# A two-layer trunk with mixture-of-experts: the dispatch steps around an expert's transposes, a later branch, a shorter rejoin of x1 and full-width norms

## The chip, the cores and the metric

The kernel runs on one core of a Trainium2 chip. The metric is the device time of one execution in microseconds (us), as a median over runs; lower is better.

## The reference

Two layers; each is a token mixer (layer 0: forgetting attention beside an S5 scan, layer 1: mLSTM) and a hierarchical mixture of experts, each followed by a layer norm of `ALPHA * h + branch`. There are 512 tokens of width 1024, 16 experts with a hidden width of 256, and two experts per token. The change touches the mixture and the norm behind it, and by shared helpers every norm:

```
for layer in range(DEPTH):
    h = layer_norm(DN_ALPHA * h + mix, ln_g[layer, 0], ln_b[layer, 0])
    ffn = hier_moe(h, ...)                       # two of 16 experts for each token
    h = layer_norm(DN_ALPHA * h + ffn, ln_g[layer, 1], ln_b[layer, 1])
...
hid = silu(t @ w_gate[e]) * (t @ w_up[e])        # 1024 -> 256, for each expert e
out = sum over e of combine[t, e] * (hid @ w_down[e])   # 256 -> 1024
layer_norm: (x - mean) * rsqrt(var + 1e-5) * g + b
```

## The kernel before

Numbers are kept as two parts. Every fp32 operand is split into a high part (a cast on ACT) and a low part (source minus high part, on DVE or POOL), and each product is three matmuls, high·high, high·low and low·high (`mm3`, L266 to L268). An expert's weights are three pieces of 1 MB, [128, 2048] fp32: two for gate and up (`gu(e)`, pieces 3e and 3e+1) and one for the down product (piece 3e+2). SP loads a piece (L247) into `raw` or one of two `ca` buffers, ACT casts the high part (L213), and the low part is subtracted at L214. Of 48 pieces of a layer POOL subtracts the down pieces of experts 1 to 13 and the pieces 42 and 45 (the first gate/up pieces of experts 14 and 15); DVE does the others.

The experts are worked on two by two. A pair (2m, 2m+1) needs the tokens of both gathered as columns: `dispatch` makes one-hot matrices on DVE (L1054, eight [128, 128] comparisons for a pair, in the pool `t`) and multiplies tokens by them on PE (L1073, 64 matmuls for a pair in four steps of 16, into `tp`), and each step's result is split (ACT and DVE, into `s` or `xr`). While a pair is computed, the next pair's dispatch runs as a generator, `prep`: four steps, two in each of the pair's experts.

For an expert e the loop of `experts` runs `gate_up(e)` (24 matmuls of 512 columns into `pj`), two steps of `prep`, then `hidden`: tanh on ACT (L1028), two elementwise steps on DVE (L1029, L1030) into `th`, and two transposes on PE (L1033, tile `sm`). The transposes are split into `pt`, and the down product follows (12 matmuls into `mm`), ACT evacuates it (L1180) into `a` and stores it to `yd` in memory (L1184).

The program is written in this order, and a scheduler decides from it, from priorities and from free buffers the order of instructions on each engine. Each engine then runs its own list in order.

At the start of `experts` stands `overflow`: each engine loads the largest count of tokens of an expert and jumps over a block that is needed only above 128 (L1210, L1211). With the last pair behind it, `gather` rebuilds `ALPHA * x1` from its two parts (`xs`, L1196 on ACT and L1197 on DVE) into `xr` and adds the stored rows of `yd` to it with eight indirect transfers of POOL (L1201). Experts 14 and 15 are not stored: their products are added from PE (L1282, L1284). `ln_sums` then does the norm of each block of 128 tokens in two halves of 512 columns: sums, Square on ACT (L314), small steps (L316, L317, L319), Identity on ACT (L323) and two steps by halves on DVE (L324, L325) of which a few go to POOL by `LN_POOL`.

Of the kernel before, what the change touches and what calls it, by code (L numbers as in the profile page):

```python
# [23 lines left out]
TWO_PI = 6.283185307179586  # L24
S5_AT = 1, 1, 2
QK_AT = 1, 3
LN_POOL = (), (0,), (0,), ()
NLAST = 2


# [21 lines left out]
class Trunk:  # L52
# [242 lines left out]
    def ln_apply(self, y, gb, mu, rs):  # L295
        V = self.nc.vector
        g, b = gb
        for i in range(2):
            h = np.s_[:, i * 512:(i + 1) * 512]
            V.scalar_tensor_tensor(y[h], y[h], mu, g[h], op0=ALU.subtract, op1=ALU.mult)  # L300
            V.scalar_tensor_tensor(y[h], y[h], rs, b[h], op0=ALU.mult, op1=ALU.add)

    def ln_sums(self, y, s, gb, pool):

        nc = self.nc
        V = nc.vector
        g, b = gb
        mu = self.sm("lnmu", [128, 1], bufs=4)
        V.tensor_scalar(mu, s[:, 0:1], s[:, 1:2], -1.0 / 1024, op0=ALU.add, op1=ALU.mult)
        yield  # L310
        q = self.sm("lns", [128, 2], bufs=4)
        for i in range(2):
            junk = self.t("t", [128, 512])
            nc.scalar.activation(junk, y[:, i * 512:(i + 1) * 512], AF.Square, bias=mu, accum_out=q[:, i:i + 1])  # L314
        ve = self.sm("lnve", [128, 1])
        V.tensor_scalar(ve, q[:, 0:1], q[:, 1:2], 1.0 / 1024, op0=ALU.add, op1=ALU.mult)  # L316
        V.tensor_scalar(ve, ve, EPS, None, op0=ALU.add)  # L317
        rs = self.rstd(ve)
        V.tensor_tensor(mu, mu, rs, op=ALU.mult)  # L319
        yield  # L320
        for i in range(2):
            h = np.s_[:, i * 512:(i + 1) * 512]
            self.last_act = nc.scalar.activation(y[h], y[h], AF.Identity, scale=rs, bias=mu)  # L323
            self.last_ln = V.tensor_tensor(y[h], y[h], g[h], op=ALU.mult)  # L324
            (nc.gpsimd if i in pool else V).tensor_tensor(y[h], y[h], b[h], op=ALU.add)  # L325
        yield


# [556 lines left out]
    def route(self, tb, layer, gb, lT, mu, rs, first):  # L885
# [77 lines left out]
                               op0=ALU.mult, op1=ALU.mult, accum_out=es)  # L963
        V.tensor_tensor(es, es, gs, op=ALU.mult)
        V.reciprocal(es, es)
        V.tensor_scalar(se, se, es, None, op0=ALU.mult)
        def scatter(r, deps=False):
            ins = nc.gpsimd.indirect_dma_start(
                out=self.cd[:, :], out_offset=bass.IndirectOffsetOnAxis(ap=pos[:, r:r + 1], axis=0),
# [47 lines left out]
    def moe_piece(self, base, i, j):  # L1017

        return self.load_piece([128, 2, 1024] if i % 3 == 2 else [128, 4, 512], *self.MOE_TAGS[j % 2],
                               "raw2" if j == 3 else self.MOE_RAW[(j - (j > 3)) % 3], at=base + i,  # L1020
                               eng=self.nc.gpsimd if i % 3 == 2 and 2 < i < 42 or i in (42, 45) else None,
                               deps=self.routed if j == 3 else (None, self.routed[1]) if j in (1, 2) else None)

    def hidden(self, gu):

        nc = self.nc
        th = self.t("t", [128, 256])
        nc.scalar.activation(th, gu[:, 0:256], AF.Tanh, scale=0.5)  # L1028
        nc.vector.scalar_tensor_tensor(th, th, 1.0, gu[:, 0:256], op0=ALU.add, op1=ALU.mult)  # L1029
        nc.vector.scalar_tensor_tensor(th, th, 0.5, gu[:, 256:512], op0=ALU.mult, op1=ALU.mult)  # L1030
        tp = self.p("sm", [128, 2, 128])
        for k in range(2):
            nc.tensor.transpose(tp[:, k, :], th[:, k * 128:(k + 1) * 128], self.ident)  # L1033
        return tp

    def tok_T(self, x):
# [91 lines left out]
    def experts(self, layer):  # L1128
        nc = self.nc
        yd = self.yd[0:2048, :].rearrange("(p e) d -> e p d", e=16)  # L1130
        base = self.piece_i
        x = []
        self.banked = []
        self.onehots(self.oh3, 3)
        self.overflow(layer, base)
        for _ in self.pair_parts(0, x):
            pass
        self.flush()
        self.sources()
        cb = self.sm("s5bc", [128, 256], bufs=1)  # L1140
        nc.sync.dma_start(cb, self.cd[0:2048, :].rearrange("(p e) c -> p (e c)", e=16))
        back, last, gus, xs, used = [], [], {}, {0: x}, iter(range(48))
        prep = None

        def gate_up(e):
            es = slice((e % 2) * 128, (e % 2 + 1) * 128)
            gus[e] = gu = self.p("pj", [128, 512])
            for q in range(2):
                w = self.moe_piece(base, 3 * e + q, next(used))
                for k in range(4):  # L1150
                    xk = xs[e // 2][q * 4 + k]
                    self.mm3(gu, xk, w, q == 0 and k == 0, q == 1 and k == 3, np.s_[:, es], np.s_[:, k, :])

        for e in range(16):
            if e % 2 == 0 and e < 14:
                xs[e // 2 + 1] = []
                prep = self.pair_parts(e // 2 + 1, xs[e // 2 + 1], back if e == 12 else None)
            if e < 15:
                gate_up(e)
            if e == 14:  # L1160
                gate_up(15)
            for _ in range(2):
                next(prep, None)
            tp = self.hidden(gus.pop(e))
            hT = (self.t("pt", [128, 2, 128], F32R), self.t("pt", [128, 2, 128], F32R))
            self.split(hT[0], hT[1], tp)
            w = self.moe_piece(base, 3 * e + 2, next(used))
            c = cb[:, 17 * e:17 * e + 1]
            if e < 16 - NLAST:
                yo = self.t("a", [128, 1024])  # L1170
            else:
                yo = (self.t("a", [128, 1024], F32R), self.t("a", [128, 1024], F32R))
                last.append(yo)
            for n in range(2):
                ns = np.s_[n * 512:(n + 1) * 512]
                ps = self.p("mm", [128, 512])
                for k in range(2):
                    self.mm3(ps, hT, w, k == 0, k == 1, np.s_[:, k, :], np.s_[:, k, ns])
                if e < 16 - NLAST:
                    nc.scalar.activation(yo[:, ns], ps, AF.Copy, scale=c)  # L1180
                else:
                    self.split(yo[0][:, ns], yo[1][:, ns], ps, scale=c)
            if e < 16 - NLAST:
                nc.scalar.dma_start(yd[e], yo)  # L1184
            if e == 15 - NLAST:
                self.gather()
                gb = self.load_ln(2 * layer + 1)
        self.piece_i += 48
        return back, last, gb

    def gather(self):

        nc = self.nc
        for tb in range(4):
            self.xr[tb] = self.t("xr", [128, 1024])
            nc.scalar.activation(self.xr[tb], self.xs[tb][0].bitcast(F32), AF.Copy, scale=ALPHA)  # L1196
            nc.vector.scalar_tensor_tensor(self.xr[tb], self.xs[tb][1].bitcast(F32), ALPHA, self.xr[tb],  # L1197
                                           op0=ALU.mult, op1=ALU.add)
        for r in range(2):
            for tb in range(4):  # L1200
                nc.gpsimd.indirect_dma_start(  # L1201
                    out=self.xr[tb], out_offset=None, in_=self.yd[:, :],
                    in_offset=bass.IndirectOffsetOnAxis(ap=self.src[:, tb, r:r + 1], axis=0),
                    compute_op=ALU.add)
# [64 lines left out]
    def moe(self, layer, done):  # L1269
# [3 lines left out]
        for tb in range(6):  # L1273
            if tb < 4:
                x = self.xr[tb]
                s = self.sm("lnsm", [128, 2], bufs=4)
                for n in range(2):
                    ns = np.s_[n * 512:(n + 1) * 512]
                    ps = self.p("pj" if n == 0 else "mm", [128, 512])
                    for i in range(NLAST):  # L1280
                        for j in range(2):
                            nc.tensor.matmul(ps, lhsT=back[i][:, tb * 128:(tb + 1) * 128], rhs=last[i][j][:, ns],  # L1282
                                             start=i + j == 0, stop=i == NLAST - 1 and j == 1)
                    nc.vector.scalar_tensor_tensor(x[:, ns], ps, 1.0, x[:, ns], op0=ALU.mult, op1=ALU.add,  # L1284
                                                   accum_out=s[:, n:n + 1])
                ln.append(self.ln_sums(x, s, gb, LN_POOL[tb]))
                next(ln[tb])
            if 0 < tb < 5:
                next(ln[tb - 1])
            if tb > 1:  # L1290
                next(ln[tb - 2])
                if tb == 2 and layer == 0:
                    self.prefetch([128, 8, 256], deps=(self.last_act, self.last_ln))
                done(tb - 2, self.xr[tb - 2])
# [304 lines left out]
```

## Time and profile before

| | |
|---|---|
| time, three runs | 1133.0, 1134.22, 1135.67 us; median 1134.22 us |
| the profiled execution | 1129.98 us, span 1127.9 us |
| mean granted clock of TensorE | 0.966 of full speed |
| busy share of the span | PE 91%, DVE 72%, ACT 50%, POOL 34% |
| experts of layer 0 | about 319 to 541 us of the span |
| experts of layer 1 | about 875 to 1102 us, then the last norm until the end |

PE is TensorE, DVE VectorE, ACT ScalarE, POOL GpSimd, and SP the queue that issues the weight loads. A row of a timeline gives the start in us from the span's start, the duration, engine, line, operation, output<-inputs and shapes; what stands in brackets at its end is the idle time of the engine just before it, and what ended it. The granted clock is the share of full speed that the chip allowed TensorE: matmuls of 512 columns then start 0.23 us apart, at half speed 0.43 us.

### The profile page before, as it was taken

Reading aid. Unit: us, or ns where it says so; the run is one execution under the profiler, and the core shown is the slowest. Engines: PE = TensorE matmul, PEld = TensorE weight load, DVE = VectorE, ACT = ScalarE, POOL = GpSimd, SP = SyncE. Lnnn points to the kernel's source line nnn. Section 1 sums busy time; section 2 is a strip of 40 time slices with the busy share of each in tenths; the row PEclk is TensorE's granted clock in tenths of the full one; section 3 lists DMA queues with packets and bytes.
Section 4 is the critical chain, followed back from the end, with each engine's and each line's share of the span. In section 5 each row is a group of like instructions: output and inputs, shape, how many; then the busy total and the mean of one; then the engine's idle time right before and its main releaser. Section 6 shows DMA issues by size and latency. Waiting matters only on the chain. (4 is left out here: it accounts for less than half of the span.)

```text
span 1127.9 us, 14810 instructions
## 1 busy us (share of the span) xinstructions
PE 1022.9 (91%) x5522; PEld 826.9 (73%) x5522; DVE 815.3 (72%) x1485; ACT 559.5 (50%) x778; POOL 379.6 (34%) x226
## 2 busy tenths in 40 slices
PE   7879999999989999997699999999999899999872
PEld 5566767767768787875577989898777787877761
DVE  7886899778776776767665766667988767767666
ACT  5123554461445665664544444444424556666744
POOL 3077546001223333345243333331012233424352
PEclk9899999999989999999799999999999899999986
DMA  6313321541257786768622222221402577868684
GB/s 227 104 58 109 127 66 46 170 170 37 114 211 249 274 291 233 287 240 248 144 75 75 76 75 75 75 76 38 150 38 114 178 267 274 313 226 297 226 218 134
DMA packets 48347, 180.62 MB, mean 160 GB/s; under 512 B 17588, under 2 KB 18516, under 8 KB 32264
## 3 DMA queue, kind: packets, MB, share of 16 engines
q1 hardware_dynamic: 41240, 156.11, 39.4%
q0 software_dynamic: 2992, 8.77, 4.0%
q10 hardware_dynamic: 4032, 14.68, 3.2%
q8 instruction: 46, 0.75, 0.3%
q14 instruction: 37, 0.30, 0.1%
HBM read 155.94 MB, written 22.42 MB: 158 GB/s over the span
## 5 line engine op out<-in xcount | busy, mean ns | idle before, releaser
L266 PE MATMUL pj<-x,wh 128*128 128x512 f32 x288 | 116.6, 406 | 7.4 <-ACT x L213 5.7
L214 POOL TENSOR_TENSOR wl<-raw,wh 128x2048 fp32r<-128x2048 f32 x15 | 69.9, 4663 | 137.2 <-ACT wh L213 137.2
L267 PE MATMUL pj<-x,wh 128*128 128x512 f32 x288 | 115.5, 401 | 0.0
L214 POOL TENSOR_TENSOR wl<-ca,wh 128x2048 fp32r<-128x2048 f32 x16 | 75.1, 4692 | 119.9 <-ACT wh L213 97.5
L213 ACT CAST wh<-raw 128x2048 fp32r<-128x2048 f32 (+1 forms) x49 | 88.2, 1801 | 53.4 <-DMA raw<-in_w 40.0
L268 PE MATMUL pj<-x,wl 128*128 128x512 f32 x288 | 114.7, 398 | 0.0
L1073 PEld LDWEIGHTS tp<-t,a 128*128 128x128 f32 x896 | 110.8, 191 | 3.0 <-ACT pt L1065 0.6
L1073 PE MATMUL tp<-t,a 128*128 128x256 f32 x896 | 111.8, 283 | 0.0
L214 POOL TENSOR_TENSOR x<-ca,x 128x2048 fp32r<-128x2048 f32 x14 | 64.6, 4618 | 135.7 <-ACT x L213 106.2
L214 DVE TENSOR_TENSOR wl<-raw,wh 128x2048 fp32r<-128x2048 f32 (+1 forms) x34 | 72.8, 2140 | 39.6 <-ACT wh L213 39.3
L214 DVE TENSOR_TENSOR wl<-ca,wh 128x2048 fp32r<-128x2048 f32 x14 | 32.1, 2292 | 60.7 <-ACT wh L213 60.7
L1180 ACT ACTIVATE a<-mm,s5bc 128x512 f32<-128x512 f32 x56 | 38.5, 687 | 73.4 <-PE mm L268 73.4
L213 ACT CAST x<-ca 128x2048 fp32r<-128x2048 f32 (+1 forms) x40 | 66.1, 1651 | 12.3 <-DMA ca<-in_w 8.4
L266 PEld LDWEIGHTS pj<-x,wh 128*128 128x128 f32 x288 | 55.4, 192 | 19.7 <-ACT x L213 6.8
L267 PEld LDWEIGHTS pj<-x,wh 128*128 128x128 f32 x288 | 54.8, 190 | 12.0 <-DVE x L214 1.8
L213 ACT CAST wh<-ca 128x2048 fp32r<-128x2048 f32 x30 | 57.1, 1904 | 13.0 <-DMA ca<-in_w 12.9
L268 PEld LDWEIGHTS pj<-x,wl 128*128 128x128 f32 x288 | 55.1, 191 | 10.7
L1054 DVE TENSOR_SCALAR t<-iota,rcm 128x128 fp32r<-128x128 f32 x112 | 58.5, 565 | 0.4
L267 PE MATMUL pj<-wl,x 128*128 128x256 f32 x192 | 56.4, 294 | 0.9 <-DVE wl L214 0.9
L268 PE MATMUL pj<-wh,x 128*128 128x256 f32 x192 | 56.2, 293 | 0.1
L266 PE MATMUL pj<-wh,x 128*128 128x256 f32 x192 | 56.2, 293 | 0.0
L281 POOL TENSOR_TENSOR lnrs<-lnve,nhalf 128x1 f32<-128x1 f32 x16 | 13.1, 818 | 126.3 <-DVE lnve L292 99.7
(488 smaller groups left out, 2869.1 us busy)
## 6 DMA issues: line engine op xcount, KB each, us to landing
raw<-in_w SPq DMA_DIRECT2D x63, 1024.0 KB, 5.2
ca<-in_w SPq DMA_DIRECT2D x62, 1024.0 KB, 5.8
yd<-a ACTq DMA_DIRECT2D x28, 512.0 KB
a<-in_ln SPq DMA_DIRECT2D x8, 512.0 KB, 6.5
a<-in_w SPq DMA_DIRECT2D x6, 512.0 KB, 6.8
yd<-t SPq DMA_DIRECT2D x6, 512.0 KB, 3.1
ca<-in_xT SPq DMA_DIRECT2D x8, 256.0 KB, 5.7
xr<-in_x SPq DMA_DIRECT2D x4, 512.0 KB, 6.3
```

What stands on the lines that cost most here:

```text
L213: a = nc.scalar.copy(h, src)
L214: b = (eng or nc.vector).tensor_sub(l, src, h.bitcast(F32))
L266: nc.tensor.matmul(ps, lhsT=aH[ai], rhs=bH[bi], start=first, stop=False)
L267: nc.tensor.matmul(ps, lhsT=aH[ai], rhs=bL[bi], start=False, stop=False)
L268: nc.tensor.matmul(ps, lhsT=aL[ai], rhs=bH[bi], start=False, stop=last)
L281: self.last_pow = self.nc.gpsimd.tensor_tensor(rs, ve, self.nhalf, op=ALU.pow)
L1054: ins = nc.vector.tensor_scalar(oh[:, j, m * 128:(m + 1) * 128], self.iota1, c[2 * i + j], None, op0=ALU.is_equal)
L1073: nc.tensor.matmul(tp[:, k, :], lhsT=self.xs[tb][i][:, cs], rhs=ohs[tb], start=tb + i == 0, stop=tb + i == 4)
L1180: nc.scalar.activation(yo[:, ns], ps, AF.Copy, scale=c)
```

## The change

It has five parts. `hidden` is cut in two, with one step of `prep` between the DVE steps and the transposes, and the other between the split of the transposes and the down product; before, both steps stood ahead of it. The branch of `overflow` is called behind expert 1. `gather` rejoins x1 in one addition on DVE, with ALPHA taken into the stored rows' scale and the norm's epsilon. The norms work on the full width: one Square on ACT, two combined steps on DVE, no Identity on ACT and nothing on POOL. Pieces 42 and 45 go from POOL to DVE.

```
     def ln_apply(self, y, gb, mu, rs):
...
+        V.scalar_tensor_tensor(y, y, mu, g, op0=ALU.subtract, op1=ALU.mult)
+        V.scalar_tensor_tensor(y, y, rs, b, op0=ALU.mult, op1=ALU.add)
...
     def ln_sums(self, y, s, gb):
...
+        junk = self.t("t", [128, 1024], BF16)
+        self.last_act = nc.scalar.activation(junk, y, AF.Square, bias=mu, accum_out=q)
+        V.scalar_tensor_tensor(y, y, mu, g, op0=ALU.add, op1=ALU.mult)
...
+        V.tensor_scalar(ve, q, 1.0 / 1024, EPS / ALPHA ** 2, op0=ALU.mult, op1=ALU.add)
         rs = self.rstd(ve)
-        V.tensor_tensor(mu, mu, rs, op=ALU.mult)
         yield
-            self.last_act = nc.scalar.activation(y[h], y[h], AF.Identity, scale=rs, bias=mu)
-            self.last_ln = V.tensor_tensor(y[h], y[h], g[h], op=ALU.mult)
-            (nc.gpsimd if i in pool else V).tensor_tensor(y[h], y[h], b[h], op=ALU.add)
+        self.last_ln = V.scalar_tensor_tensor(y, y, rs, b, op0=ALU.mult, op1=ALU.add)
...
-                               eng=self.nc.gpsimd if i % 3 == 2 and 2 < i < 42 or i in (42, 45) else None,
+                               eng=self.nc.gpsimd if i % 3 == 2 and 2 < i < 42 else None,
...
-        self.overflow(layer, base)                       # experts, ahead of the first pair
...
-            for _ in range(2):
-                next(prep, None)
-            tp = self.hidden(gus.pop(e))
+            th = self.hidden_act(gus.pop(e))
+            next(prep, None)
+            tp = self.hidden_T(th)
             hT = (self.t("pt", [128, 2, 128], F32R), self.t("pt", [128, 2, 128], F32R))
             self.split(hT[0], hT[1], tp)
+            next(prep, None)
             w = self.moe_piece(base, 3 * e + 2, next(used))
...
+            if e == 1:
+                self.overflow(layer, base)
...
-            nc.scalar.activation(self.xr[tb], self.xs[tb][0].bitcast(F32), AF.Copy, scale=ALPHA)
-            nc.vector.scalar_tensor_tensor(self.xr[tb], self.xs[tb][1].bitcast(F32), ALPHA, self.xr[tb],
-                                           op0=ALU.mult, op1=ALU.add)
+            nc.vector.tensor_tensor(self.xr[tb], self.xs[tb][0].bitcast(F32), self.xs[tb][1].bitcast(F32), op=ALU.add)
```

Below stands what this does to the lists of DVE and PE in the pair (4, 5) of layer 0. On DVE before, from expert 4's steps (`t_4430`) to the one-hots of the next dispatch (`t_4616`), which come behind expert 5's first step:

```order
L214 TENSOR_TENSOR x_934_4468<-ca_4466,x_933_4467 128x2048
L214 TENSOR_TENSOR wl_4486<-raw_4484,wh_4485 128x2048
L214 TENSOR_TENSOR s_917_4406<-tp_4388,s_916_4405 128x512
L1029 SCALAR_TENSOR_TENSOR t_4430<-t_4430,pj_4341 128x256
L1030 SCALAR_TENSOR_TENSOR t_4430<-t_4430,pj_4341 128x256
L214 TENSOR_TENSOR s_920_4427<-tp_4409,s_919_4426 128x512
L214 TENSOR_TENSOR pt_4438<-sm_4434,pt_4437 128x256
L214 TENSOR_TENSOR wl_4582<-ca_4580,wh_4581 128x2048
L1029 SCALAR_TENSOR_TENSOR t_4544<-t_4544,pj_4465 128x256
L1054 TENSOR_SCALAR t_4616<-iota_130,rcm_2778 128x128
L1030 SCALAR_TENSOR_TENSOR t_4544<-t_4544,pj_4465 128x256
L1054 TENSOR_SCALAR t_4616<-iota_130,rcm_2778 128x128
```

On DVE in the changed kernel, at the same two weight pieces and expert 4's steps (now `t_4370`, L1024 and L1025; the one-hots are `t_4374` and `t_4379`, L1052):

```order
L213 TENSOR_TENSOR x_934_4460<-ca_4458,x_933_4459 128x2048
L213 TENSOR_TENSOR wl_4478<-raw_4476,wh_4477 128x2048
L1024 SCALAR_TENSOR_TENSOR t_4370<-t_4370,pj_4333 128x256
L1052 TENSOR_SCALAR t_4374<-iota_130,rcm_2776 128x128
L1025 SCALAR_TENSOR_TENSOR t_4370<-t_4370,pj_4333 128x256
L1052 TENSOR_SCALAR t_4374<-iota_130,rcm_2776 128x128
L1052 TENSOR_SCALAR t_4374<-iota_130,rcm_2917 128x128 x2
L1052 TENSOR_SCALAR t_4379<-iota_130,rcm_3059 128x128 x2
L1052 TENSOR_SCALAR t_4379<-iota_130,rcm_3262 128x128 x2
L213 TENSOR_TENSOR pt_4409<-sm_4405,pt_4408 128x256
```

The run of eight one-hots has moved from the odd expert to the even one, to just behind (and around) the steps whose result PE transposes. On PE before, at expert 4's transposes (`sm_4434`; the dispatch ahead of them ends with `tp_4409`, and its one-hots `t_4378` and `t_4383` were made in the pair before):

```order
L1073 MATMUL tp_4409<-t_4383,a_3235 128x256
L1073 MATMUL tp_4409<-t_4383,a_3236 128x256
L266 MATMUL pj_4465<-x_933_4467,xr_4171 128x512
L267 MATMUL pj_4465<-x_934_4468,xr_4171 128x512
L268 MATMUL pj_4465<-x_933_4467,xr_4172 128x512
L266 MATMUL pj_4465<-x_933_4467,xr_4171 128x512
L1033 MATMUL sm_4434<-ident,t_4430 128x128 x2
L267 MATMUL pj_4465<-x_934_4468,xr_4171 128x512
L268 MATMUL pj_4465<-x_933_4467,xr_4172 128x512
L266 MATMUL pj_4465<-x_933_4467,xr_4171 128x512
L267 MATMUL pj_4465<-x_934_4468,xr_4171 128x512
L266 MATMUL mm_4448<-wh_4442,pt_4437 128x512
```

On PE in the changed kernel, at the same transposes (`sm_4405`), with the last matmuls of gu(5) (`pj_4457`) that are put ahead of them:

```order
L265 MATMUL pj_4457<-wh_4477,xr_4279 128x512
L266 MATMUL pj_4457<-wl_4478,xr_4279 128x512
L267 MATMUL pj_4457<-wh_4477,xr_4280 128x512
L265 MATMUL pj_4457<-wh_4477,xr_4279 128x512
L1031 MATMUL sm_4405<-ident,t_4370 128x128 x2
L1071 MATMUL tp_4384<-t_4374,a_2744 128x256
L1071 MATMUL tp_4384<-t_4374,a_2745 128x256
L1071 MATMUL tp_4412<-t_4374,a_2744 128x256
L1071 MATMUL tp_4384<-t_4374,a_2886 128x256
L1071 MATMUL tp_4384<-t_4374,a_2887 128x256
L1071 MATMUL tp_4412<-t_4374,a_2745 128x256
L1071 MATMUL tp_4384<-t_4379,a_3027 128x256
```

The 32 matmuls of the dispatch now stand between the transposes and the down product (which follows the 32nd of them), and they read the one-hots `t_4374` and `t_4379` that DVE makes in the rows above. Sixteen matmuls of gu(5) stand ahead of the transposes, where there were four. In the odd expert the other two steps (32 matmuls) stand behind the even expert's down product and eight matmuls of gu(5), with four matmuls of gu(6) between them and the transposes. On PE in the changed kernel the branch (L1208, L1209) stands inside the down product of expert 1 (`mm_3559`, `mm_3567`):

```order
L267 MATMUL pj_4099<-wh_4101,s_724_3407 128x512
L265 MATMUL mm_3559<-x_755_3553,pt_3527 128x512
L266 MATMUL mm_3559<-x_756_3554,pt_3527 128x512
L265 MATMUL mm_3567<-x_755_3553,pt_3527 128x512
L1208 TENSOR_LOAD rmc_3285
L1209 COMPARE_AND_BRANCH
```

Before, it stood ahead of the last L1109 matmuls in front of gu(0).

## Rows read from the trace of the kernel before

**Rows 1.** Windows: busy time of each engine in the experts of layer 0.

```profile
320.00:541.00 221.00, 203.06 (x1078) 168.95 (x1077) 147.25 (x183) 131.92 (x142) 84.62 (x24) 0.98 0.75 260
```

**Rows 2.** PE's waits, 312 to 530 us: total, times, longest.

```profile
PE mm L268 <- DVE pt L214: 6.1, 4, 2.1
```

**Rows 3.** Timeline of PE: transposes of experts 2, 4, 6 and 12; one expert's dispatch matmuls.

```profile
357.48 0.38 PE L1033 MATMUL sm<-ident,t 128*128 128x128 f32 x2
...
364.68 3.98 PE L1073 MATMUL tp<-t,a 128*128 128x256 f32 x32
...
382.80 0.38 PE L1033 MATMUL sm<-ident,t 128*128 128x128 f32 x2
...
409.28 0.44 PE L1033 MATMUL sm<-ident,t 128*128 128x128 f32 x2
...
494.24 0.38 PE L1033 MATMUL sm<-ident,t 128*128 128x128 f32 x2
```

**Rows 4.** Timeline of PE at the branch and the start of gu(0), layer 0.

```profile
316.45 0.98 PE L1109 MATMUL mm<-pt,a 128*128 128x256 f32 x3 [3.62 <-PEq L1211]
...
318.94 0.63 PE L266 MATMUL pj<-wh,xr 128*128 128x512 f32 x1
...
321.29 0.40 PE L266 MATMUL pj<-wh,xr 128*128 128x512 f32 x1
...
325.02 0.40 PE L267 MATMUL pj<-x,xr 128*128 128x512 f32 x1
```

**Rows 5.** Lines of DVE, 351 to 489 us (experts 2 to 11).

```profile
L1054 DVE TENSOR_SCALAR t<-iota,rcm 128x128 fp32r<-128x128 f32 x40 | 23.2, 631 | 0.0
```

**Rows 6.** DVE, layer 0: the tile `t` by lines, 300 to 560 us.

```profile
L1054 DVE TENSOR_SCALAR t<-iota,rcm x56: 270/278/3446, 320.9 to 483.7; 128x128 fp32r<-128x128 f32 x56
```

**Rows 7.** Timeline of POOL: subtractions of the down pieces.

```profile
357.11 4.61 POOL L214 TENSOR_TENSOR x<-ca,x 128x2048 fp32r<-128x2048 f32 x1 [11.07 <-DVE t L1030]
369.72 5.75 POOL L214 TENSOR_TENSOR wl<-ca,wh 128x2048 fp32r<-128x2048 f32 x1 [8.00 <-ACT wh L213]
384.87 4.59 POOL L214 TENSOR_TENSOR x<-ca,x 128x2048 fp32r<-128x2048 f32 x1 [9.39 <-ACT x L213]
...
410.21 4.61 POOL L214 TENSOR_TENSOR x<-ca,x 128x2048 fp32r<-128x2048 f32 x1 [7.81 <-ACT x L213]
```

**Rows 8.** Timeline of DVE around one collision with a POOL subtraction.

```profile
368.73 2.29 DVE L214 TENSOR_TENSOR x<-raw,x 128x2048 fp32r<-128x2048 f32 x1
...
372.46 3.10 DVE L1054 TENSOR_SCALAR t<-iota,rcm 128x128 fp32r<-128x128 f32 x1
```

**Rows 9.** Timeline of DVE: the first step of expert 2.

```profile
356.23 0.41 DVE L1029 SCALAR_TENSOR_TENSOR t<-t,pj 128x256 f32<-128x256 f32 x1
```

**Rows 10.** Timeline of PE after a wait of 4 us.

```profile
518.68 0.54 PE L267 MATMUL pj<-x,s 128*128 128x512 f32 x1 [4.00 <-DVE x L214]
...
522.43 0.39 PE L267 MATMUL pj<-x,s 128*128 128x512 f32 x1
```

**Rows 11.** Timeline of DVE in the tail of layer 1.

```profile
1068.39 1.21 DVE L1197 SCALAR_TENSOR_TENSOR xr<-a,xr 128x1024 f32<-128x1024 f32 x1
...
1073.66 6.40 DVE L214 TENSOR_TENSOR x<-raw,x 128x2048 fp32r<-128x2048 f32 x1
...
1109.38 0.69 DVE L1284 SCALAR_TENSOR_TENSOR xr<-pj,xr 128x512 f32<-128x512 f32 x1 [0.73 <-DMA xr<-yd,rsrc]
```

**Rows 12.** Timeline of POOL: the gathers of layer 1.

```profile
1081.79 1.94 POOL L1201 DMA_INDIRECT xr<-yd,rsrc  x1 [3.89 <-DMA yd<-a]
...
1092.67 1.54 POOL L1201 DMA_INDIRECT xr<-yd,rsrc  x1 [3.34 <-DMA xr<-yd,rsrc]
```

**Rows 13.** Lines of DVE, 1109 to 1128 us.

```profile
L324 DVE TENSOR_TENSOR xr<-xr,a 128x512 f32<-128x512 f32 x8 | 5.4, 682 | 0.0
L325 DVE TENSOR_TENSOR xr<-xr,a 128x512 f32<-128x512 f32 x6 | 4.0, 688 | 0.1
L319 DVE TENSOR_TENSOR lnmu<-lnmu,lnrs 128x1 f32<-128x1 f32 x4 | 2.7, 683 | 1.4 <-POOL lnrs L281 1.4
```

More of the change, by code (lines that the diff above doesn't have):

```diff
@@ L26 @@
 QK_AT = 1, 3
-LN_POOL = (), (0,), (0,), ()
 NLAST = 2
@@ L297, in ln_apply, with ln_sums @@
         g, b = gb
[L298 to L303, printed above, removed]
+        V.scalar_tensor_tensor(y, y, mu, g, op0=ALU.subtract, op1=ALU.mult)
+        V.scalar_tensor_tensor(y, y, rs, b, op0=ALU.mult, op1=ALU.add)
+    def ln_sums(self, y, s, gb):
         nc = self.nc
@@ L310, in ln_sums @@
         yield
[L311 to L314, printed above, removed]
+        q = self.sm("lns", [128, 1], bufs=4)
+        junk = self.t("t", [128, 1024], BF16)
+        self.last_act = nc.scalar.activation(junk, y, AF.Square, bias=mu, accum_out=q)
+        V.scalar_tensor_tensor(y, y, mu, g, op0=ALU.add, op1=ALU.mult)
         ve = self.sm("lnve", [128, 1])
-        V.tensor_scalar(ve, q[:, 0:1], q[:, 1:2], 1.0 / 1024, op0=ALU.add, op1=ALU.mult)
-        V.tensor_scalar(ve, ve, EPS, None, op0=ALU.add)
+        V.tensor_scalar(ve, q, 1.0 / 1024, EPS / ALPHA ** 2, op0=ALU.mult, op1=ALU.add)
         rs = self.rstd(ve)
-        V.tensor_tensor(mu, mu, rs, op=ALU.mult)
         yield
-        for i in range(2):
-            h = np.s_[:, i * 512:(i + 1) * 512]
-            self.last_act = nc.scalar.activation(y[h], y[h], AF.Identity, scale=rs, bias=mu)
-            self.last_ln = V.tensor_tensor(y[h], y[h], g[h], op=ALU.mult)
-            (nc.gpsimd if i in pool else V).tensor_tensor(y[h], y[h], b[h], op=ALU.add)
+        self.last_ln = V.scalar_tensor_tensor(y, y, rs, b, op0=ALU.mult, op1=ALU.add)
         yield
@@ L965, in route @@
         V.reciprocal(es, es)
-        V.tensor_scalar(se, se, es, None, op0=ALU.mult)
+        V.tensor_scalar(se, se, es, 1.0 / ALPHA, op0=ALU.mult, op1=ALU.mult)
         def scatter(r, deps=False):
@@ L1020, in moe_piece, with hidden_act @@
                                "raw2" if j == 3 else self.MOE_RAW[(j - (j > 3)) % 3], at=base + i,
-                               eng=self.nc.gpsimd if i % 3 == 2 and 2 < i < 42 or i in (42, 45) else None,
+                               eng=self.nc.gpsimd if i % 3 == 2 and 2 < i < 42 else None,
                                deps=self.routed if j == 3 else (None, self.routed[1]) if j in (1, 2) else None)
     def hidden(self, gu):
+        return self.hidden_T(self.hidden_act(gu))
+    def hidden_act(self, gu):
         nc = self.nc
@@ L1030, in hidden, with hidden_T @@
         nc.vector.scalar_tensor_tensor(th, th, 0.5, gu[:, 256:512], op0=ALU.mult, op1=ALU.mult)
+        return th
+    def hidden_T(self, th):
         tp = self.p("sm", [128, 2, 128])
         for k in range(2):
-            nc.tensor.transpose(tp[:, k, :], th[:, k * 128:(k + 1) * 128], self.ident)
+            self.nc.tensor.transpose(tp[:, k, :], th[:, k * 128:(k + 1) * 128], self.ident)
         return tp
@@ L1285, in moe @@
                                                    accum_out=s[:, n:n + 1])
-                ln.append(self.ln_sums(x, s, gb, LN_POOL[tb]))
+                ln.append(self.ln_sums(x, s, gb))
                 next(ln[tb])
```

## The prediction

> **What bounds the kernel now.** I read the windows first: in the 221 us of layer 0's experts PE is busy for 203 us, at a granted clock of 0.98, and no other engine for more than 147 us [rows 1]. So PE's own list sets the pace, and I read its timeline next. The transposes of expert 2 start at 357.48 and those of expert 12 at 494.24: five pairs in 136.8 us, 27.4 us each [rows 3]. What must PE do in a pair? 72 matmuls of 512 columns (48 for gate and up, 24 for the two down products), which start 0.233 us apart (321.29 to 325.02, 16 steps [rows 4]), 16.8 us; and two groups of 32 dispatch matmuls of 3.98 us [rows 3], 8.0 us. With the transposes about 25 us. So a pair has 2.4 us to lose or win at most, 12 us for a layer's five full pairs. PE's largest wait, 6.1 us in four, is at the third matmul of a down product, for the low part of the transposed hidden values, `pt` [rows 2]. The reader should look at why that part is late.
>
> DVE's lines tell it: 40 one-hot comparisons took 0.631 us on average [rows 5], but the median of the same line is 0.278 us and the longest 3.446 us [rows 6]. So each of the five runs of eight held one blocked comparison: 40 times (0.631 - 0.278) is 14.1 us, 2.8 us for each run. The timeline names the partner. POOL began a subtraction at 369.72 and ended it at 375.47; the comparison that DVE began at 372.46 ended at 375.56 [rows 7, 8]. POOL's own operation took 5.75 us instead of 4.61, because DVE was in a subtraction until 371.02 when it began [rows 7, 8]. Whichever of the two is under way, the other waits for its end.
>
> A page of the Trainium skill, "SBUF — State Buffer", section "Who interferes with whom", says that DVE and GpSimd share one port pair, that a DVE instruction of the tensor_scalar kind or with two SBUF inputs contends for it, and that whoever issues first has it for the whole instruction. By that rule the same run would cost nothing if it were issued first, and POOL would wait instead; the trace shows both orders (3.10 us on DVE, 1.1 us on POOL [rows 7, 8]).
>
> In before this collision is cheap, since the run's one-hots are for the next pair's dispatch; only `pt` queued behind the run is late, in odd experts.
>
> **The dispatch step.** The gain it can have: 32 dispatch matmuls lie between the transposes and the down product, so that `pt` has 4 us to be split and PE's waits of rows 2 go. If nothing else waited, a pair would lie between 25 us (all waits gone) and 27.4 (none); I take 26.0, since only the `pt` waits are addressed: -1.4 us.
>
> But the orders show a new dependence. Those 32 matmuls read one-hots that DVE makes around L1024 and L1025 of the same expert, just ahead of use, where before they had been made in the pair before. So a blocked comparison now stops PE with nothing left to run: the transposes, the dispatch and the down product stand behind it in order. Does POOL's subtraction fall there? In both kernels it waits for ACT's cast of the odd expert's down piece, which ACT runs behind the even expert's tanh. In before's expert 2, DVE's first step starts at 356.23 and POOL at 357.11, 0.9 us later [rows 7, 9]. Placed in the new order from that first step, the run of eight lasts at most to +3.0 us (two steps of 0.41 and eight comparisons of 0.278 [rows 6, 9]); as such operations overlap by some hundredths each, I take +2.3. So POOL begins within the run. Measured from the transposes of the even expert, POOL starts at -0.37 in expert 2, +2.07 in expert 4, and +0.93 in expert 6 [rows 3, 7]; experts 8 and 10 lie between 2 and 6. The transposes come about 1.1 us behind the first step, so that the run would end at about +1.2 from them. Four of five start inside it; expert 4 escapes, because its piece landed late.
>
> Price of one collision: POOL's 4.61 us from a start that lies 0 to 2.3 us into the run, so the run ends 2.3 to 4.6 us late, and I take 3.6 (a start about 1.3 us into it, between the 0.9 of expert 2 and the 2 of expert 6). PE then waits about that long, and it comes back slow: behind the wait of 4.00 us at 518.68 nine matmuls took 3.75 us instead of 2.10 [rows 10], behind that of 3.62 us at the branch the first 2.35 us of gu(0) held 6 matmuls worth 1.40, with the L1109 ahead slower still [rows 4]. So +1.65 to 2.1; I take 1.9. A collision costs 5.5 us (bounds 2.3, where the wait is too short to slow the clock, and 6.7).
>
> Pairs: five per layer from expert 1's down product on, with nothing colliding 5 × -1.4 = -7.0; the sixth run, for the last pair, stands in a stretch where order and tail shift against each other, and I put it at +0.4 without a collision. With 12 possible collisions in the kernel (six a layer), each adds 5.5.
>
> **The branch.** PE's idle time at L1109 is 3.62 us and it runs slow behind it [rows 4]. That stays; it moves. At the start the gain is small, about 2 us, as gu(0) waits for its piece's high and low parts anyway. In expert 1's down product nothing covers it: 3.6 + 1.9 = 5.5 us. Queued behind it are ACT's evacuation, and SP's loads behind its own jump. Net +3.5 us a layer (bounds +1.5, if the piece is not what gu(0) waits for, and +5.5).
>
> **The tail.** The first gather is issued at 1081.79, and the fifth one (1092.67) waited for the first to land [rows 12]; two weight loads, freed late because DVE's subtraction took 6.40 us against POOL's of piece 45, share the memory with it [rows 11]. With piece 45 on DVE and L1196 gone, the subtraction takes 2.3 and the loads precede the gathers. I put the first landing at 5 us behind its issue instead of 10: -4.9 (bounds 0 and -7). The last gather's data is used at 1109.38 [rows 11]; from there DVE works through eight L324, six L325 and four L319, 12.1 us [rows 13]. In their place stand at most seven full-width steps of 1.21 us (the price of L1197, a two-input step of that width [rows 11]), 8.5 us: -3.3 (bounds -2 and -5). The narrow norm ahead of the experts gains 0.7. The rest of gather's ACT work is off the path. Together -8.9 a layer.
>
> **Sum.** Without collisions, a layer: -7.0 + 0.4 + 3.5 - 8.9 = -12.0, the kernel -24. With c collisions: -24 + 5.5c. It breaks even between 4 and 5 of 12. Four of five in the rows above would be 9 or 10; I take 9, since POOL could be held off by a DVE subtraction or a late landing: -24 + 49.5 = +25.5 us. Against the profiled 1129.98 that is 1155.5; this execution lies 4.2 us under the median of the runs, so 1160 for the median.
>
> **Rivals.** *The run goes first (faster).* If the down piece lands late, as in expert 4, or if DVE's back-to-back operations keep POOL out, the one-hots are made before the subtraction and nobody on PE waits: 0 to 2 collisions, -24 to -13, 1110 to 1121. It decides at about 2.3 us from the first step: a POOL start behind that costs nothing. For it speaks expert 4 [rows 3, 7]; against it that the longer pairs of a colliding order give the pieces more time to land. By the page's rule above this is the case of DVE issued first. *The pace is not PE's (faster).* POOL takes a down piece in every 13.3 us on average (357.11 to 410.21, four steps [rows 7]) through one buffer, so load, cast and subtraction could hold a pair at 27.4 whatever PE's order is; then the pairs give 0 in place of -7.0 and nothing collides at cost: -5.0 a layer, 1124. *Half and half.* 4 to 6 collisions: -2 to +9, 1132 to 1143. *All 12 collide at the full 6.7:* -24 + 80 = +56, 1190; at 5.5 it is +42, 1176.
>
> **How the numbers follow.** Most runs collide (7 to 12): 0.57, from 1149 to 1176, likeliest 1160. None or few: 0.22. Pace held elsewhere: 0.11. Half and half: 0.10. About 0.2% (2.3 us) is what a measurement of this kernel can tell from no change; of half and half 0.05 falls inside it, 0.01 below and 0.04 above. So faster 0.34, same 0.05, slower 0.61. The range takes in both signs: 1112 to 1180; for the likeliest case alone 1146 to 1178.
>
> **What would show it.** Right: comparisons at L1052 with a longest of 3 to 4.6 us in the even experts, PE idle 2 to 4 us at the first L1071 matmuls or the L1031 transposes, released by DVE, with a granted clock below 1 behind it, and transposes of even experts about 31 us apart where they collide, 26 where not. PE idle some 3.6 us in expert 1's down product. First gather landing about 5 us after its issue. Wrong: POOL's L213 beginning behind the run, or PE's waits at L1071 under 1 us; then the time ends near 1115. The tail could be mis-sized by 2 to 4 us a layer without touching the sign.

## The result, and the profile after

The changed kernel takes 1195.24 us (median of 4 runs, 1192.04 to 1198.86), the kernel before 1134.95: a ratio of 1.0538, interval 1.0497 to 1.0579. It is slower, as forecast, but by 60 us in place of 25, and outside the range. Ratios and intervals, here and below, are of executions in the usual, faster state; the medians beside them are of all. The profiled execution (span 1197.1 us) holds some 7 us that are not the change's: at 150 to 202 us, in layer 0's mixer, its granted clock was 0.84 where before had 1.00, and work that took before 45 us there took 52. So I read stages, not the span.

The same window as in [rows 1], with the experts some 7 us further on, shows PE busy for 190.64 us in place of 203.06, at a granted clock of 0.90 in place of 0.98:

```profile
320.00:541.00 221.00, 190.64 (x958) 162.30 (x957) 138.01 (x171) 114.40 (x124) 63.69 (x16) 0.90 0.63 225
```

PE's waits in layer 1's experts (900 to 1150 us; total, times, longest). The wait for `pt` of [rows 2] is gone; five waits for one-hots, one for the elementwise steps, one at the transposes of the last pair's one-hots (L1060) and the branch (L1209) stand in its place:

```profile
PE tp L1071 <- DVE t L1052: 18.5, 5, 3.9
PE mm L267 <- PEq L1209: 4.5, 1, 4.5
PE sm L1031 <- DVE t L1025: 3.9, 1, 3.9
PE tp L1060 <- DVE t L1052: 3.6, 1, 3.6
```

One pair, layer 1, expert 6. PE's timeline first, then DVE's and POOL's. POOL (4.56 us) begins half a microsecond after DVE has begun the run of seven comparisons; the run, 1.46 us where nothing holds it, takes 5.72. PE does six dispatch matmuls, stands for 3.78 us, and the other 26 take 4.90 us, where [rows 3] has 3.98 for all 32:

```profile
1027.78 0.38 PE L1031 MATMUL sm<-ident,t 128*128 128x128 f32 x2
1027.92 0.95 PE L1071 MATMUL tp<-t,a 128*128 128x256 f32 x6
1032.65 4.90 PE L1071 MATMUL tp<-t,a 128*128 128x256 f32 x26 [3.78 <-DVE t L1052]
```

```profile
1026.42 0.41 DVE L1024 SCALAR_TENSOR_TENSOR t<-t,pj 128x256 f32<-128x256 f32 x1
1026.75 0.28 DVE L1052 TENSOR_SCALAR t<-iota,rcm 128x128 fp32r<-128x128 f32 x1
1026.94 0.42 DVE L1025 SCALAR_TENSOR_TENSOR t<-t,pj 128x256 f32<-128x256 f32 x1
1027.28 5.72 DVE L1052 TENSOR_SCALAR t<-iota,rcm 128x128 fp32r<-128x128 f32 x7
1032.91 0.41 DVE L213 TENSOR_TENSOR pt<-sm,pt 128x256 fp32r<-128x256 f32 x1
```

```profile
1027.76 4.56 POOL L213 TENSOR_TENSOR x<-ca,x 128x2048 fp32r<-128x2048 f32 x1 [7.29 <-ACT x L212]
```

The transposes of experts 2 and 12 of layer 0 (PE's timeline, as in [rows 3]) are now (524.04 - 371.61) / 5 = 30.5 us apart per pair, in place of 27.4. One run of layer 0 escaped: in expert 4 (403.06) the subtraction began at 403.93, and the comparisons had taken 1.46 us:

```profile
371.61 0.38 PE L1031 MATMUL sm<-ident,t 128*128 128x128 f32 x2
...
403.06 0.38 PE L1031 MATMUL sm<-ident,t 128*128 128x128 f32 x2
...
524.04 0.27 PE L1031 MATMUL sm<-ident,t 128*128 128x128 f32 x1
```

Counted over both layers, 13 of 14 runs (seven a layer, the first pair's included; there it is a small step between the comparisons that is held) were held by a subtraction of POOL.

### The profile page after: what moved, and what is told of

It reads as the page before. It is cut to its first block, busy times and chain, and to the rows that moved or that the text cites. A ratio compares the mean times of both kernels' runs of the same rounds, so it can differ in the third digit from the quotient of the medians.

```text
span 1197.1 us, 14715 instructions
## 1 busy us (share of the span) xinstructions
PE 1055.1 (88%) x5522; PEld 859.4 (72%) x5522; DVE 825.1 (69%) x1445; ACT 538.3 (45%) x738; POOL 355.9 (30%) x218
## 5 line engine op out<-in xcount | busy, mean ns | idle before, releaser
L1071 PE MATMUL tp<-t,a 128*128 128x256 f32 x896 | 137.3, 320 | 25.6 <-DVE t L1052 25.6
L1071 PEld LDWEIGHTS tp<-t,a 128*128 128x128 f32 x896 | 134.0, 228 | 29.1 <-DVE t L1052 27.1
L213 POOL TENSOR_TENSOR wl<-ca,wh 128x2048 fp32r<-128x2048 f32 x12 | 55.2, 4599 | 176.4 <-DVE t L1025 103.2
L213 DVE TENSOR_TENSOR x<-ca,x 128x2048 fp32r<-128x2048 f32 (+1 forms) x26 | 46.6, 1797 | 69.2 <-ACT x L212 69.2
L1052 DVE TENSOR_SCALAR t<-iota,rcm 128x128 fp32r<-128x128 f32 x112 | 71.6, 700 | 0.0
L280 POOL TENSOR_TENSOR lnrs<-lnve,nhalf 128x1 f32<-128x1 f32 x16 | 18.9, 1182 | 134.8 <-DVE lnve L291 103.5
L1178 ACT ACTIVATE a<-mm,s5bc 128x512 f32<-128x512 f32 x56 | 37.2, 687 | 41.0 <-PE mm L267 40.9
```

What stands on the lines that cost most here:

```text
L213: b = (eng or nc.vector).tensor_sub(l, src, h.bitcast(F32))
L280: self.last_pow = self.nc.gpsimd.tensor_tensor(rs, ve, self.nhalf, op=ALU.pow)
L1052: ins = nc.vector.tensor_scalar(oh[:, j, m * 128:(m + 1) * 128], self.iota1, c[2 * i + j], None, op0=ALU.is_equal)
L1071: nc.tensor.matmul(tp[:, k, :], lhsT=self.xs[tb][i][:, cs], rhs=ohs[tb], start=tb + i == 0, stop=tb + i == 4)
```

## The experiments

In each set the kernel before ran beside the others (median 1131 to 1132 us), the changed kernel did not run again. So where a run is compared with the changed kernel or with a run of another set, the text takes how far each lies from the kernel before of its own set.

**What carries the loss.** The dispatch steps undone, the rest kept:

```
-            th = self.hidden_act(gus.pop(e))
...
+            for _ in range(2):
+                next(prep, None)
+            tp = self.hidden(gus.pop(e))
...
```

> The changed kernel with both dispatch steps put back ahead of the two elementwise steps; branch behind expert 1, one-addition rejoin, full-width norms and pieces 42 and 45 on DVE stay. If the steps carry the loss by whatever way (collision or order): 1130 to 1145 us, the pairs back at about 27.4 us. If the branch behind expert 1 carries it: 1180 us or more, with a wait of PE at the branch of 4 us and long slow stretches behind it.

1133.19 us, ratio 0.9995 (0.9951 to 1.0039): no difference to before. The steps alone, on the kernel before:

> The kernel before with only the dispatch steps moved. If the steps carry the loss: 1180 to 1200 us, pairs of about 31 us, one blocked comparison of 4 to 5 us in nearly every run of one-hots and PE waiting 3 to 4 us for it. If the branch or the other parts carry it: within 10 us of 1134.

1176.99 us, 1.0391 (1.0332 to 1.045). So the steps carry the loss, 46 us alone; the other parts add some 14 us beside them and nothing without them. The traces show where those 14 us may lie: with the steps alone POOL holds 10 of the 14 runs, in the changed kernel 13, which is 4.6 us for each held run in either kernel.

**Collision or order?** All down pieces on DVE:

```
-  eng=self.nc.gpsimd if i % 3 == 2 and 2 < i < 42 else None
+  eng=None
```

> The changed kernel with every down piece's low part subtracted on DVE, so that POOL does nothing during the experts and no comparison can be held by it; DVE gets 13 subtractions of 2.29 us more a layer. If the collision is the cause: comparisons never above 0.3 us, PE's waits for them gone, pairs of 26 to 28 us, 1115 to 1145 us. If the order on PE itself (16 matmuls ahead of the transposes, 32 behind them) lengthens the pair: pairs stay at 30 us or more, 1175 us or more.

1166.65 us, 1.0283 (1.0219 to 1.0347): neither. The comparisons run at 0.280 us and no PE wait names them, but pairs take 28.7 us (experts 2 to 12 of layer 0, as above). The timelines of DVE, ACT and PE show what came instead. The even piece (`wl<-ca`) stands ahead of `pt`, for which PE does not stand still. ACT casts the next gate piece only behind the evacuation of the down product (L1178), DVE subtracts it behind that, and PE waits 1.17 us for the one and 1.82 us for the other. In layer 0 such waits for a gate piece are 14.8 us in ten. That the even pieces on DVE bring this about is shown further on, where they are back on POOL; by which step they do is not:

```profile
1019.23 2.28 DVE L213 TENSOR_TENSOR wl<-ca,wh 128x2048 fp32r<-128x2048 f32 x1
1021.43 0.42 DVE L213 TENSOR_TENSOR pt<-sm,pt 128x256 fp32r<-128x256 f32 x1
1024.14 2.29 DVE L213 TENSOR_TENSOR wl<-raw,wh 128x2048 fp32r<-128x2048 f32 x1 [2.29 <-ACT wh L212]
1027.33 2.29 DVE L213 TENSOR_TENSOR x<-ca,x 128x2048 fp32r<-128x2048 f32 x1 [0.90 <-ACT x L212]
```

```profile
1024.01 1.50 ACT L1178 ACTIVATE a<-mm,s5bc 128x512 f32<-128x512 f32 x2
1025.40 1.89 ACT L212 CAST x<-ca 128x2048 fp32r<-128x2048 f32 x1
```

```profile
1027.35 0.51 PE L265 MATMUL pj<-x,xr 128*128 128x512 f32 x1 [1.17 <-ACT x L212]
1029.67 0.50 PE L266 MATMUL pj<-x,xr 128*128 128x512 f32 x1 [1.82 <-DVE x L213]
```

The one-hots written ahead of the gate products (the edit in outline):

```
     prep = self.pair_parts(...)
+    next(prep)          # dispatch yields once behind its one-hots
```

> The changed kernel with the eight one-hots of a pair written ahead of the even expert's gate and up products instead of behind its tanh, nothing else changed; on DVE they then stand in the expert before. POOL still subtracts and may still collide with them. If lateness of the one-hots at their use is the cause: the blocked comparisons stay, PE's waits for them go, pairs of 26 to 27.5 us, 1105 to 1135 us. If any collision costs, or the order on PE does: 1170 us or more.

1144.57 us, 1.0119 (1.008 to 1.0159): 47 of the 60 us are back, with pairs of 28.0 us. No comparison was held (0.278 us on average in layer 0's pairs), so this run cannot tell lateness from collision, as it was meant to. DVE's weight pieces are held in their place, for one form 2.90 us on average in place of 2.29, and PE's largest waits of the stage are for `pt` from ACT:

```profile
L213 DVE TENSOR_TENSOR wl<-raw,wh 128x2048 fp32r<-128x2048 f32 x5 | 14.5, 2898 | 7.6 <-ACT wh L212 7.6
```

The one-hots left late, and POOL's subtraction made to wait instead (in outline):

```
+  # odd experts' down pieces
+  tc.add_manual_dep(<POOL subtraction>, <last one-hot>, Sync)
```

> The changed kernel with one wait added: POOL's subtraction of each odd expert's down piece waits for the last one-hot of the run that it used to hold up. DVE's work and all lists stay as they are. If the collision alone makes the loss: no comparison above 0.3 us, pairs of 26 to 27.5 us, 1125 to 1140 us. If the order has a second limit behind it, the first gate piece of the odd expert (its buffer is held until the odd down product before it ends, and only 16 matmuls now cover its cast and subtraction): pairs of 29 to 30 us, PE waiting 1 to 2 us for x from ACT or DVE at the first matmuls of the odd expert, 1155 to 1175 us.

1132.66 us, 1.0021 (0.9998 to 1.0044). One wait, of an engine that is not the bound, takes back all of the loss. POOL now begins behind the run, and none of the 14 runs is held (POOL and DVE in expert 2 of layer 0):

```profile
362.41 4.63 POOL L214 TENSOR_TENSOR x<-ca,x 128x2048 fp32r<-128x2048 f32 x1 [15.61 <-DVE t L1057]
```

```profile
360.72 1.46 DVE L1057 TENSOR_SCALAR t<-iota,rcm 128x128 fp32r<-128x128 f32 x7
```

But pairs take (498.21 - 361.08) / 5 = 27.4 us (PE's transposes of experts 2 and 12), no less than in the kernel before:

```profile
361.08 0.38 PE L1036 MATMUL sm<-ident,t 128*128 128x128 f32 x2
...
498.21 0.27 PE L1036 MATMUL sm<-ident,t 128*128 128x128 f32 x1
```

My second limit, the late first gate piece, is there (PE waits 6.8 us in five for x from DVE in layer 0) but small. Two shortened subtractions in the kernel without POOL tested it from the other side (one execution each):

> The kernel without POOL's subtractions once more, and of the first gate piece of each odd expert only 64 of 2048 columns are subtracted; the product takes the high part in place of the low one, so the sums are rougher. DVE's chain from that piece to PE is 2.2 us shorter. If that chain is the second limit: pairs fall from 29.5 to 27 us or less, PE's wait for x from DVE goes, 1125 to 1145 us. If not: 29 us or more, 1155 us or more.

> The counterpart: the same shortening on the second gate piece of each even expert, so DVE has the same relief of 2.2 us a pair at another place. If the chain of the odd expert's first piece is the second limit: pairs of 28.5 us or more, 1150 us or more. If DVE's sum of work is the limit: the same as with the odd expert's piece, within 5 us.

1119.62 and 1133.02 us: a gain at either place, 13 us more at the odd expert's first piece. In both, PE also no longer waits for a low part of the shortened piece, and the kernel before alone spreads over 9 us (1126.2 to 1135.3). So that both DVE's sum and that chain count in the kernel without POOL is suggested, not shown.

**The odd pieces alone on DVE.**

```
-  eng=self.nc.gpsimd if i % 3 == 2 and 2 < i < 42 else None
+  eng=self.nc.gpsimd if i % 6 == 2 and 2 < i < 42 else None
```

> The changed kernel with the low part of the odd experts' down pieces alone subtracted on DVE (7 a layer), those of the even ones on POOL. If the collision with the odd piece is the whole loss and DVE has room for 2.29 us a pair: 1130 to 1140 us, as with the waiting subtraction. If DVE's added work costs as much as in the kernel without POOL: 1150 us or more.

1124.23 us, 0.9929 (0.9901 to 0.9957): 8 us faster than the kernel before, and so 68 us below the changed kernel. PE's transposes of experts 2 and 12 of layer 0, (490.48 - 359.51) / 5 = 26.2 us a pair, and DVE's line of the comparisons:

```profile
359.51 0.38 PE L1031 MATMUL sm<-ident,t 128*128 128x128 f32 x2
...
490.48 0.27 PE L1031 MATMUL sm<-ident,t 128*128 128x128 f32 x1
```

```profile
L1052 DVE TENSOR_SCALAR t<-iota,rcm 128x128 fp32r<-128x128 f32 x40 | 8.7, 285 | 0.0
```

DVE's added 2.29 us a pair lie behind `pt`, where it has room. From the kernel without POOL this one differs by the even pieces alone, so they were the ones that had no room on DVE.

**The branch.** Put back to the start, in the changed kernel:

> The changed kernel with the branch put back to the start of the experts; steps, rejoin, norms and pieces 42 and 45 as in the changed kernel. By my sum the branch costs 3.5 us a layer in its new place: 7 us less than the changed kernel, about 1188 us. If its place costs nothing: 1195 us.

1180.17 us (1.0452, 1.0384 to 1.0519), 12 us less. But its trace also has three held runs fewer, 10 of 14 in place of 13. In expert 2 of layer 0, for one, the comparisons end at 364.13; POOL begins at 364.05 and is itself held, by DVE's next subtraction, to 6.76 us in place of 4.6 (DVE's timeline, then POOL's):

```profile
363.07 1.06 DVE L1052 TENSOR_SCALAR t<-iota,rcm 128x128 fp32r<-128x128 f32 x5
364.05 2.28 DVE L213 TENSOR_TENSOR wl<-raw,wh 128x2048 fp32r<-128x2048 f32 x1
```

```profile
364.05 6.76 POOL L213 TENSOR_TENSOR x<-ca,x 128x2048 fp32r<-128x2048 f32 x1 [9.36 <-ACT x L212]
```

Three held runs at 4.6 us are 14 us, the whole difference. So what the branch's place costs among collisions is not shown by this run; it may be no more than the order of DVE that comes with it. Moved alone, on the kernel before:

> The kernel before with only the branch moved behind expert 1. By my sum (3.5 us a layer): 1141 us beside 1134. If its cost needs the moved steps (15 us between the changed kernel and the one with the branch put back): within 3 us of the kernel before.

1132.58 us, 1.0013 (0.9982 to 1.0045). Put back where the odd pieces are on DVE:

> The odd experts' down pieces on DVE as in the last run, and the branch put back to the start of the experts. If the branch behind expert 1 costs 3.5 us a layer by itself: 1117 us beside 1124. If its place costs nothing: within 3 us of 1124.

1117.95 us, 0.9875 (0.9844 to 0.9907). Beside the kernel before of each set that is 5 us below the same kernel with the late branch (6.3 by the medians alone), near the sum's 7; the two intervals overlap at their ends, so this is a rough figure.

**The tail.** Rejoin, norms and pieces 42 and 45 alone:

> The kernel before with only the rejoin in one addition, the full-width norms and pieces 42 and 45 on DVE. By my sum (8.9 us a layer): 1116 us. If the gathers gain nothing, since loads of weights and of the norm's rows now stand ahead of the last store that they wait for, only the norm is left: 3 us a layer or less, 1128 us or more, the last gather landing as far behind the transposes of expert 13 as before (38.7 us in layer 1).

1134.11 us, 1.0033 (1.0004 to 1.0061). PE's transposes of expert 13 and POOL's first gather in layer 1: 14.9 us apart, where before had 11.2 (1070.59 to 1081.79). A sooner landing is there (the fifth gather, at 1094.35, no longer waits for the first, so that has landed within 8.8 us of its issue, where before took almost 11), the gather itself starts 3.7 us later, and the two nearly cancel. Before, then the tail alone:

```profile
1070.59 0.44 PE L1033 MATMUL sm<-ident,t 128*128 128x128 f32 x2 [1.59 <-DVE t L1030]
```

```profile
1070.67 0.38 PE L1031 MATMUL sm<-ident,t 128*128 128x128 f32 x2
```

```profile
1085.59 1.61 POOL L1197 DMA_INDIRECT xr<-yd,rsrc  x1 [26.38 <-DMA yd<-a]
```

SP's queue shows what moved: two weight pieces and the norm's two rows now go out between the transposes and the last store, which ACT issues at 1077.35, 8.2 us ahead of the gather. Before, the norm's rows went at 1067.5 and 1068.2 and the weights at 1080, behind a store issued at 1078.28, 3.5 us ahead of the gather:

```profile
1072.41 0.33 SPq L246 DMA_DIRECT2D raw<-in_w  x1
1072.79 0.42 SPq L273 DMA_DIRECT2D a<-in_ln  x1
1073.31 0.38 SPq L275 DMA_DIRECT2D a<-in_ln  x1
1074.95 0.33 SPq L246 DMA_DIRECT2D ca<-in_w  x1
```

That these transfers delay the store which the gathers wait for is what the order of events suggests. The load of the norm's rows written sooner (`load_ln` behind expert 9):

> As the tail alone, and the load of the norm's rows is written behind expert 9 in place of expert 13, which takes one of its two transfers off the stretch ahead of the last store. If transfers ahead of that store delay the gathers: the first gather starts 1 to 3 us sooner behind the store, and the time is 2 to 6 us below the tail alone. If not: the same.

1132.47 us, 1.0003 (0.9973 to 1.0032), no different from the tail alone; the order around it changed too, and the gather started 7.5 us behind the store, 0.7 us sooner, but not sooner behind the transposes. The cause of the later gather stays open.

**Waits in other orders.** The waiting subtraction with the branch put back:

> The changed kernel with POOL's subtraction waiting for the one-hots and the branch put back to the start: both costs that the runs so far name taken out. If they add: 8 to 15 us below the 1133 us of the waiting subtraction alone, 1118 to 1125 us, faster than the kernel before. If the branch only costs together with the collisions: 1130 us or more.

1175.4 us, 1.0388 (1.0339 to 1.0437): a plain miss. With the branch elsewhere the list of DVE came out differently: the gate piece `wl<-raw` stood behind the run, with `pt` behind it. POOL, set free by the run's end, started first, and that piece took 4.73 us in place of 2.29 (timelines of POOL and DVE, and PE's waits in layer 0):

```profile
481.45 4.60 POOL L214 TENSOR_TENSOR x<-ca,x 128x2048 fp32r<-128x2048 f32 x1 [9.60 <-DVE t L1057]
```

```profile
480.12 1.07 DVE L1057 TENSOR_SCALAR t<-iota,rcm 128x128 fp32r<-128x128 f32 x5
483.47 4.73 DVE L214 TENSOR_TENSOR wl<-raw,wh 128x2048 fp32r<-128x2048 f32 x1 [2.28 <-ACT wh L213]
488.12 0.68 DVE L214 TENSOR_TENSOR xr<-tp,xr 128x512 fp32r<-128x512 f32 x1
488.72 0.41 DVE L214 TENSOR_TENSOR pt<-sm,pt 128x256 fp32r<-128x256 f32 x1
```

```profile
PE mm L271 <- DVE pt L214: 17.2, 4, 4.3
```

The same wait on the kernel before, and there with the tail:

> The kernel before, with POOL's subtraction of each even expert's down piece made to wait for the last one-hot of the run that it collides with there. If that collision costs little in the kernel before, because its one-hots are made a pair ahead: within 4 us of 1131, with PE's wait for the low part of the transposed values gone or smaller. If it also costs there: 8 to 15 us faster.

> The tail alone (rejoin, norms, pieces 42 and 45) on the kernel before's steps, with the same wait: 3 us or less beside the kernel with the wait alone if the tail gains nothing, 10 us or more below it if it does.

1144.02 us (1.0112, 1.0074 to 1.015) and 1151.33 us (1.0186, 1.0133 to 1.024): both worse, and the tail gains nothing beside the wait either. In the first, subtractions of DVE took 2.8 to 4.2 us in place of 2.29 in most pairs, and PE's waits for `pt` from ACT in layer 0 grew from 3.0 to 10.1 us, while those for its low part from DVE went. That the held subtractions make the loss here too is likely, not shown. The collision taken out on the kernel before, by the pieces that collide there:

```
-  eng=self.nc.gpsimd if i % 3 == 2 and 2 < i < 42 or i in (42, 45) else None
+  eng=self.nc.gpsimd if i % 6 == 5 and 2 < i < 42 or i in (42, 45) else None
```

> The kernel before, with the even experts' down pieces, the ones that hold up its one-hots, subtracted on DVE. If the collision is cheap there, as the forecast said: no gain over 3 us, rather a loss from DVE's added work. If the same change pays there as it does behind the moved steps: 1120 us or less, and the moved steps gain nothing.

1113.72 us, 0.9836 (0.9802 to 0.987), the fastest of all. Its pairs of layer 0 take (488.49 - 357.68) / 5 = 26.2 us, as with the moved steps and the odd pieces on DVE. No comparison is held (0.279 us on average; in the kernel before 12 runs held one), and PE's wait for `pt` of [rows 2] falls from 6.1 to 2.5 us. PE's timeline, DVE's line of the comparisons, PE's wait:

```profile
357.68 0.38 PE L1033 MATMUL sm<-ident,t 128*128 128x128 f32 x2
...
488.49 0.38 PE L1033 MATMUL sm<-ident,t 128*128 128x128 f32 x2
```

```profile
L1054 DVE TENSOR_SCALAR t<-iota,rcm 128x128 fp32r<-128x128 f32 x40 | 9.1, 279 | 0.0
```

```profile
PE mm L268 <- DVE pt L214: 2.5, 3, 0.9
```

## Why the prediction was right in sign and wrong in size

*The mechanism* held. The one-hots, made just ahead of use, are held by POOL's subtraction, PE has nothing left to run, and it comes back slow. Either cure of this one collision takes back 59 us (the wait) or 68 us (the other engine), and the kernels with 13 held runs (the changed one), 10 (two of them) and none (the wait) lie 60, 46 to 48 and 1 to 2 us above the kernel before.

*The step that failed* is the sum without collisions, -24 us: two of its terms, the pairs and the tail, did not come. Of the 35 us by which the forecast of +25.5 fell short, about 25 lie there and about 10 in the collisions, 59 in place of 49.5.

*The count* was 13 of 14, not 9 of 12. Of the prediction's own 12 runs 11 were held; besides, it left out the first pair of each layer, where POOL held one of the small steps between the comparisons. "Four of five" was read from an order with 27 us a pair. The prediction had itself named against the first rival that longer pairs give the pieces time to land, and did not use it; whether that is the reason is not shown, since with the steps alone, at 30.9 us a pair, 4 of 14 runs escape.

*The price*, 5.5 us, was near: 4.6 us where 13 or 10 runs are held, 5.2 by the cure on the other engine. Its working was not. A start 1.3 us into the run gives 4.61 - 1.3 = 3.3 by its own rule, not 3.6, and the trace does not follow that rule: the seven comparisons take 5.5 to 6.0 us in place of 1.46 whether POOL starts 0.3 us ahead of them or 0.6 us into them. That 3.6 lies near PE's waits (3.78 us in the pair above) was luck.

*The -7.0 us a layer* for the pairs did not come from the steps. With the wait, where no comparison is held, a pair takes 27.4 us as before. With the odd pieces on DVE it takes 26.2 us (forecast 26.0), but it does so with the old order too, once that order's own collision is gone. So most of PE's waits for `pt` [rows 2] were not due to the place of the dispatch: they were the price of the collision in the kernel before. "In before this collision is cheap" is the sentence that failed; taking that collision out is worth 17 us there. A part of the 17 may be the shorter subtraction (2.29 us on DVE, 4.61 on POOL), which no run separates. Moving the steps gains nothing that these runs show: with either order's colliding pieces on DVE and the branch at the start, the moved steps and the tail stand at 1117.95 us, the old order at 1113.72.

*The branch*, 3.5 us a layer, is some 2.5 to 3.2 where nothing collides and not measurable alone on the kernel before (+0.1%). The 12 us that it makes among the collisions go with three more held runs, which the sum did not connect with it.

*The tail*, -8.9 us a layer, is the largest error: its three parts measure +0.3% (0.0 to 0.6) together, not -1.6%. Its term of -4.9 for a sooner first landing counted the gather from its issue, and held the issue fixed; the issue moved back by 3.7 us. Its -3.3 for the last norm is 12.1 - 8.5 = 3.6 by its own rows, for at most seven full-width steps; the tail alone has eight of 1.27 us, 10.2 us, and from the last gather's use (1108.37) to DVE's last step it takes 14.1 us where before took 15.0.

So in place of -24 + 49.5: with the collision taken out by the wait the rest stands at about +1 to +2, not at -24, and the collisions give 59. The sign came out right because the collisions outweigh both errors, which went the same way.

The rule of the Trainium skill, "SBUF — State Buffer", section "Who interferes with whom", that the first to issue has the shared pair for its whole instruction, agrees with the 5.72 us run here and with the 4.73 us piece in the kernel with the wait and the branch put back. By it a wait on POOL can hand the conflict to the next DVE instruction that uses the pair; the trace of the waiting subtraction with the branch put back shows that, while with the first list of DVE none of the 128x2048 subtractions in layer 0's experts took over 2.4 us.

## What to carry to other kernels

When a step is moved next to its consumer, ask what its producer can be held by: 1.5 us of comparisons became 5.7, and the slack that had hidden this was what the move used up. A long subtraction on POOL is paid by what stands in DVE's list when it starts; give DVE the pieces that collide and POOL those that fall where DVE reads PE's results (`tp`, `sm`), and read both in the new order's trace, since a wait that cures one list harms another. Before a wait of the bound engine is put down to the order, look whether an operation ahead of it takes longer than its median.

## What the runs showed of the hardware

A held instruction can be tiny. In the changed kernel's first pair, layer 0, DVE's step on 128 by 8 numbers took 4.00 us, to the end of POOL's subtraction (334.58 to 339.12); the same step of layer 1, not held, took 0.16 us (DVE's timeline):

```profile
335.14 4.00 DVE L999 TENSOR_SCALAR rsr<-rrow 128x8 f32<-128x8 f32 x1
```

DVE's steps with one operand in PE's results were not held. In the kernel with the waiting subtraction POOL subtracts from 362.41 to 367.04, and DVE's two steps on `tp` inside that time take 0.69 us each, as such a step does with POOL idle (0.69 us at 1036.01 in the changed kernel):

```profile
364.38 0.69 DVE L214 TENSOR_TENSOR xr<-tp,xr 128x512 fp32r<-128x512 f32 x1 [1.87 <-ACT xr L213]
365.95 0.69 DVE L214 TENSOR_TENSOR xr<-tp,xr 128x512 fp32r<-128x512 f32 x1 [0.87 <-ACT xr L213]
```
